# Two transformer blocks on one core: in the second mixer every second weight split, and the row operations after two norms, go from VectorE to GpSimd

## The chip, the cores and the metric

The kernel runs on one core of one Trainium2 chip. The metric is device time in microseconds from start to end of one execution, as the median of several runs; lower is better. The profile's own rows give times from the start of its span.

## The reference

Two blocks work on one sequence of 256 tokens of width 1024, in float32, with batch 1 and one layer each. The first has a mixer of sliding-window attention and a chunked mLSTM, then a gated feed-forward of hidden width 2816. The second, in which the change lies, is cut here to what matters:

```python
x = layer_norm(x, emb_ln_g, emb_ln_b)
sh1, sc1, gt1, sh2, sc2, gt2 = split(silu(c) @ w_ada + b_ada, 6)
h = x * (1 + sc1) + sh1
p = h @ w_in
y_a = gmlp_spatial_gating(p[..., :1024], ...)      # gelu, norm, a 128 x 128 mix over tokens
y_b = rwkv7_time_mix(p[..., 1024:], ...)           # 8 heads, a state update per token
x = layer_norm(ALPHA * x + gt1 * (concat(y_a, y_b) @ w_out), ln1_g, ln1_b)
h = x * (1 + sc2) + sh2
gu = h @ w_ffn_in
x = layer_norm(ALPHA * x + gt2 * ((silu(gu_left) * gu_right) @ w_ffn_out), ln2_g, ln2_b)
```

## The kernel before, in words

**Products in three parts.** Every large product is made exact to nearly float32 by splitting both operands into a high and a low part and adding three matmuls (mm3: high by high, high by low, low by high). The activations are split once; the weights stream in from memory in slots of 128 partitions by 1024 columns (512 KB).

**What happens to a slot (load, lines 787 to 813).** SyncE issues the transfer into one of six buffers named raw. ScalarE casts raw to the high part whi (line 809). VectorE subtracts, wlo = raw - whi (line 810). Then raw is free, and both parts go to TensorE. There are three places for whi and wlo; some phases add places in other tiles (there the high and low parts are named wx, xhi and xlo). stream (line 826) keeps two slots loaded ahead of the job that is emitted. Before the plan starts, the first mixer has its own split (line 422) that the change does not touch.

**The order of work.** From the end of the first mixer on, the order on all engines is written out at build time by a planner (Plan, from line 68). Every instruction is given a cost (cost, line 279), threads have ranks, and each engine is given the instruction of lowest rank among those ready at the simulated time. A planned instruction is never interrupted, and on the chip each engine runs its list strictly in that order, so that one that must wait holds up all behind it on its engine. The splits have level 5 (on engines other than TensorE), the threads of the second mixer 1 to 3, the norms that carry the residual 0 to 0.5, the row operations 5. The planner books an elementwise operation on VectorE at 0.06 us and on GpSimd at 0.44 us, plus one column per 1/960 us on either. Every instruction that is emitted through the planner is shown by the profile at line 376.

**The second mixer (phase "m2").** set_phase gives the phase its name after the last matmul of the first feed-forward has been emitted. From then on the stream splits what is left of four value slots, then three slots of the low-rank gates (one of 256 columns), four of k and r for each of two head groups, four of v, four of the gate branch (gmlp), eight of w_out and the first ones of the next feed-forward's w_ffn_in. Two threads run the recurrence of one head group each: rwkv_pre, rwkv_gram, rwkv_base (a 16 x 16 substitution of 15 steps on VectorE, whose blocks go through memory as "images" on SyncE's queue), rwkv_levels, rwkv_state and rwkv_out. A third, gmlp, may only start at the event m2.x.

**The row operations (row_affine, line 1055).** After a norm, the next product needs only the normalised x, with gain and bias folded into the modulation. The residual needs x times gain plus bias itself; row_affine does that afterwards, two blocks of 128 tokens by two halves of 512 columns by a multiplication and an addition: eight instructions on VectorE. It runs twice: after the embedding norm in the second mixer (it starts when the r of the second head group is there and sets m2.x at its end), and after the norm ln1 at the start of the second feed-forward (it sets f2.x, which the gate's thread and the last norm's rows wait for).

**GpSimd before the change.** It holds the reciprocal square roots of all norms (rsq, a power of -0.5 on a few columns: rms_r, ln_r, hr_r), masks at setup, clears of small tiles and the transfers of rows that are copied to all partitions (brow, sgrow, mix, lora).

Of the kernel before, what the change touches and what calls it, by code (L numbers as in the profile page):

```python
# [8 lines left out]
F32 = mybir.dt.float32  # L9
# [4 lines left out]
ALU = mybir.AluOpType  # L14
# [19 lines left out]
class Pool:  # L34
# [3 lines left out]
    def __init__(self, pool, **bufs):  # L38
        self.pool, self.bufs = pool, bufs
# [349 lines left out]
class Builder:  # L389
    def __init__(self, tc, io, out):  # L390
        self.tc, self.nc, self.io, self.out = tc, tc.nc, io, out
        self.plan = None


    def bg_add(self, job, rate):
# [391 lines left out]
    def load(self, view, kt, cols, place):  # L787

        nc, n = self.nc, kt * cols
        raw = self.wraw.tile([P, n], F32, tag="raw", name="raw")  # L790
        self.plan.level = 5
        nc.sync.dma_start(raw.rearrange("p (k n) -> p k n", k=kt), view)
        cut = [slice(i, min(n, i + 512)) for i in range(0, n, 512)]
        if place in ("x", "t2"):
            pairs = []
            for c in cut:
                hi, lo = (self.ph.tile([P, 512], F32R, tag=place, name="x" + s) for s in ("hi", "lo"))
                nc.scalar.copy(hi, raw[:, c])
                nc.vector.tensor_tensor(lo, raw[:, c], hi.bitcast(F32), op=ALU.subtract)
                pairs.append((hi, lo))  # L800
            self.plan.drop(raw)
            self.plan.level = None
            return pairs, place
        if place == "hT":
            t = self.act.tile([P, 2, 1024], F32R, tag="hT", name="wx")
            hi, lo = t[:, 0, 0:n], t[:, 1, 0:n]
        else:
            hi, lo = (self.wsp.tile([P, n], F32R, tag=s, name=s) for s in ("whi", "wlo"))
        nc.scalar.copy(hi, raw)
        nc.vector.tensor_tensor(lo, raw, hi.bitcast(F32), op=ALU.subtract)  # L810
        self.plan.drop(raw)
        self.plan.level = None
        return [(hi[:, c], lo[:, c]) for c in cut], place
# [241 lines left out]
    def row_affine(self, gb, ev):  # L1055
        for b in range(NB):
            for h in range(2):
                s = slice(h * 512, (h + 1) * 512)
                for i, op in enumerate((ALU.mult, ALU.add)):
                    self.nc.vector.tensor_tensor(self.x[:, b, s], self.x[:, b, s], gb()[i][:, s], op=op)  # L1060
                yield
        self.plan.set(ev)

# [1374 lines left out]
```

## Time and profile before

| | |
|---|---|
| median of 3 runs | 831.02 us (830.13 to 833.05) |
| profiled execution | 836.26 us, its span 834.5 us |
| instructions in the span | 14958 |
| TensorE matmul busy | 784.6 us (94%) |
| TensorE weight load busy | 674.4 us (81%) |
| VectorE (DVE) busy | 581.3 us (70%), 1032 instructions |
| ScalarE (ACT) busy | 379.8 us (46%), 599 instructions |
| GpSimd (POOL) busy | 63.3 us (8%), 143 instructions |
| mean granted TensorE clock | 0.975 of full |
| moved from memory | 175.06 MB, 213 GB/s over the span |

The profile shows one execution; its time is a little above the median of the runs without a profile. An engine's busy time doesn't say whether anything waited for it: that is read from the chain of work that ended last and from the waits. Names in a row stand as out<-in; buffer numbers are left out, and digits in names of inputs too (in_ln_g is ln1_g_2 or ln2_g_2).

### The profile page before, as it was taken

What the parts mean: (1) busy time and instruction counts of PE and PEld (TensorE: products, weight loads), DVE (VectorE), ACT (ScalarE), POOL (GpSimd) and SP (SyncE); (2) the same over time, 40 slices, a digit from 0 to 9 for tenths busy, and PEclk for the clock granted to TensorE, in tenths of its full rate; (3) what the DMA queues carried; (4) which work ended last, traced back from release to release, by engine and by line L of the source; (5) the groups of instructions that cost most, each with busy time, mean ns of one, the idle gap of its engine ahead of it and who ended that gap; (6) DMA issues with size and microseconds to landing.
All of it is one profiled execution on the core that took longest, in us unless ns stands there. A gap on an engine that the chain in (4) does not pass through costs nothing.

```text
span 834.5 us, 14958 instructions
## 1 busy us (share of the span) xinstructions
PE 784.6 (94%) x5912; PEld 674.4 (81%) x5912; DVE 581.3 (70%) x1032; ACT 379.8 (46%) x599; POOL 63.3 (8%) x143
## 2 busy tenths in 40 slices
PE   5999899999979999999998999998897999999995
PEld 4778467899857999998875878876675899999884
DVE  3468866877678977876456467988549778667446
ACT  4346854454554444445425574443235444445330
POOL 3014010100020310000001011000101000000000
PEclk9999999999989999999999999999997999999999
DMA  9996489796759999997659618677434769966711
GB/s 273 318 280 179 159 290 281 208 247 179 245 160 307 272 307 262 305 303 243 186 168 261 165 51 199 155 232 219 153 103 156 219 191 293 251 200 202 254 51 51
DMA packets 205078, 178.94 MB, mean 214 GB/s; under 512 B 24052, under 2 KB 171712, under 8 KB 205008
## 3 DMA queue, kind: packets, MB, share of 16 engines
q1 hardware_dynamic: 201456, 168.37, 69.8%
q0 software_dynamic: 3552, 9.63, 3.5%
q8 instruction: 46, 0.75, 0.4%
q14 instruction: 24, 0.20, 0.1%
HBM read 175.06 MB, written 2.90 MB: 213 GB/s over the span
## 4 chain that ended last, share of the span: by engine, by line
PE 78%; DVE 8%; DMA 5%; ACT 3%; issue 3%; POOL 2%; SPq 1%; DVEq 0%; ACTq 0%; POOLq 0%
PE mm L376 51%; PE sm L376 6%; PE mm L434 4%; PE mm L435 4%; PE mm L436 4%; DMA raw<-in_w_in_dram 2%; PE ad L554 1%; DVE x L376 1%; POOL hr_r L376 1%; DMA base<-image 1%; PE ad L376 1%; DMA ada_raw<-in_w_ada_dram 1%; SPq L376 1%; DMA raw<-in_w_ffn_gate_dram 1%; DVE wlo L376 1%
## 5 line engine op out<-in xcount | busy, mean ns | idle before, releaser
L376 DVE TENSOR_TENSOR wlo<-raw,whi 128x1024 fp32r<-128x1024 f32 (+1 forms) x135 | 164.0, 1218 | 103.2 <-ACT whi L376 102.3
L376 ACT CAST whi<-raw 128x1024 fp32r<-128x1024 f32 (+1 forms) x135 | 140.9, 1045 | 190.3 <-PE mm L376 153.6
L376 PE MATMUL mm<-f_lo,whi 128*128 128x256 f32 x560 | 156.8, 280 | 0.0
L376 PE MATMUL mm<-f_hi,wlo 128*128 128x256 f32 x560 | 156.5, 279 | 0.0
L376 PE MATMUL mm<-f_hi,whi 128*128 128x256 f32 x560 | 156.1, 279 | 0.0
L376 PEld LDWEIGHTS mm<-f_lo,whi 128*128 128x128 f32 x560 | 105.9, 189 | 0.6 <-issue 0.5
L376 PEld LDWEIGHTS mm<-f_hi,whi 128*128 128x128 f32 x560 | 105.5, 188 | 0.3 <-issue 0.2
L376 PEld LDWEIGHTS mm<-f_hi,wlo 128*128 128x128 f32 x560 | 105.2, 188 | 0.7 <-issue 0.7
L427 DVE TENSOR_TENSOR wlo<-raw,whi 128x1024 fp32r<-128x1024 f32 x42 | 51.3, 1220 | 24.2 <-ACT whi L426 24.2
L426 ACT CAST whi<-raw 128x1024 fp32r<-128x1024 f32 x42 | 44.0, 1049 | 45.4 <-DMA raw<-in_w_in_dram 21.1
L434 PE MATMUL mm<-h_hi,whi 128*128 128x256 f32 (+1 forms) x184 | 52.8, 287 | 0.8 <-ACT qkv L1390 0.8
L436 PE MATMUL mm<-h_hi,wlo 128*128 128x256 f32 (+1 forms) x184 | 51.5, 280 | 0.0
L435 PE MATMUL mm<-h_lo,whi 128*128 128x256 f32 (+1 forms) x184 | 51.5, 280 | 0.0
L376 PE MATMUL mm<-m_hi,wlo 128*128 128x256 f32 (+1 forms) x152 | 43.2, 289 | 0.2
L376 PE MATMUL mm<-m_hi,whi 128*128 128x256 f32 (+1 forms) x152 | 42.9, 286 | 0.3 <-DVE kT L376 0.3
L376 PE MATMUL mm<-m_lo,whi 128*128 128x256 f32 (+1 forms) x152 | 42.6, 283 | 0.4 <-DVE vT L376 0.4
L434 PEld LDWEIGHTS mm<-h_hi,whi 128*128 128x128 f32 (+1 forms) x184 | 34.4, 187 | 3.1 <-ACT qkv L1390 1.7
L435 PEld LDWEIGHTS mm<-h_lo,whi 128*128 128x128 f32 (+1 forms) x184 | 34.1, 186 | 0.5 <-issue 0.5
L436 PEld LDWEIGHTS mm<-h_hi,wlo 128*128 128x128 f32 (+1 forms) x184 | 34.2, 186 | 0.0
L376 DVE SCALAR_TENSOR_TENSOR part<-ada_raw,cs,part 128x512 f32<-128x512 f32 x42 | 31.4, 748 | 0.6
L376 PE MATMUL mm<-wlo,hid_hi 128*128 128x512 f32 x80 | 31.3, 391 | 0.0
L376 PE MATMUL mm<-whi,hid_hi 128*128 128x512 f32 x80 | 31.2, 390 | 0.0
(548 smaller groups left out, 1784.0 us busy)
## 6 DMA issues: line engine op xcount, KB each, us to landing
ada_raw<-in_w_ada_dram SPq DMA_DIRECT2D x96, 512.0 KB, 6.0
raw<-in_w_in_dram SPq DMA_DIRECT2D x60, 512.0 KB, 5.4
raw<-in_w_ffn_in_dram SPq DMA_DIRECT2D x44, 512.0 KB, 5.0
raw<-in_w_ffn_gate_dram SPq DMA_DIRECT2D x22, 512.0 KB, 6.0
raw<-in_w_ffn_up_dram SPq DMA_DIRECT2D x22, 512.0 KB, 6.0
raw<-in_w_ffn_down_dram SPq DMA_DIRECT2D x22, 512.0 KB, 5.8
raw<-in_w_ffn_out_dram SPq DMA_DIRECT2D x22, 512.0 KB, 4.1
raw<-in_w_out_dram SPq DMA_DIRECT2D x16, 512.0 KB, 4.3
```

The costliest lines, as they stand in the source:

```text
L376: return lambda *args, **kw: self.plan.issue(self.name, op, args, kw, lambda: f(*args, **kw))
L426: self.nc.scalar.copy(hi, raw)
L427: self.nc.vector.tensor_tensor(lo, raw, hi.bitcast(F32), op=ALU.subtract)
L434: mm(out, lhsT=l[0], rhs=r[0], start=start, stop=False)
L435: mm(out, lhsT=l[0], rhs=r[1], start=False, stop=False)
L436: mm(out, lhsT=l[1], rhs=r[0], start=False, stop=stop)
L554: nc.tensor.matmul(ps[32 * g:32 * g + 32, :], lhsT=cv["rep"][:, 2 * (s - 1) + g, :], rhs=raws[s - 1 + g // 2][:, g % 2, :], start=s == 1, ...
```

## The change

Two lines change their engine. In load, a flag self.odd turns over at every slot of the ordinary kind that is split while the phase is "m2", beginning with true; where it is true, GpSimd does the subtraction, elsewhere VectorE as before. Outside that phase the flag is false. In row_affine all eight operations of both norms go to GpSimd. The planner sees the new engine and books it by its own cost, so the written order of all engines may differ from the one before.

```diff
     def __init__(self, tc, io, out):
         self.tc, self.nc, self.io, self.out = tc, tc.nc, io, out
-        self.plan = None
+        self.plan, self.odd = None, False
...
         nc.scalar.copy(hi, raw)
-        nc.vector.tensor_tensor(lo, raw, hi.bitcast(F32), op=ALU.subtract)
+
+        self.odd = self.phase == "m2" and not self.odd
+        (nc.gpsimd if self.odd else nc.vector).tensor_tensor(lo, raw, hi.bitcast(F32), op=ALU.subtract)
         self.plan.drop(raw)
...
                 for i, op in enumerate((ALU.mult, ALU.add)):
-                    self.nc.vector.tensor_tensor(self.x[:, b, s], self.x[:, b, s], gb()[i][:, s], op=op)
+                    self.nc.gpsimd.tensor_tensor(self.x[:, b, s], self.x[:, b, s], gb()[i][:, s], op=op)
                 yield
```

## Rows read from the trace of the kernel before

**Rows 1.** Busy by stretch: stretch, length, each engine's us (instructions), clock, DMA share, GB/s.
```profile
439.00:640.00 201.00, 182.21 (x1751) 147.11 (x1744) 139.78 (x309) 89.92 (x162) 18.62 (x21) 0.96 0.60 166
640.00:835.00 195.00, 185.47 (x1239) 168.71 (x1237) 131.07 (x162) 77.37 (x95) 3.86 (x6) 0.98 0.65 193
```

**Rows 2.** The page: chain that ended last, share of the span by engine.
```profile
PE 78%; DVE 8%; DMA 5%; ACT 3%; issue 3%; POOL 2%; SPq 1%; DVEq 0%; ACTq 0%; POOLq 0%
```

**Rows 3.** The chain's pieces in the mixer (start, us, what), and its line for 540:580.
```profile
by line: SPq L376 14.2%; DMA raw<-in_w_out_dram 12.8%; PE sm L376 11.9%; DVE vv L376 8.2%; PE mm L376 7.8%; DVE gl_t L376 6.7%; issue 6.3%; DVE wlo L376 6.1%; PE ad L376 5.4%; ACT whi L376 5.3%; DVE base L376 4.4%; DVE W L376 3.5%; ACT gl_t
...
489.73 2.61 POOL hr_r L376
...
560.04 1.05 ACT whi L376
561.12 1.23 DVE wlo L376
```

**Rows 4.** Waits in 439 to 640: who waited for whom, us, times, longest.
```profile
DVE wlo L376 <- ACT whi L376: 19.9, 13, 4.2
...
PE sm L376 <- DVE x L376: 4.8, 2, 2.8
PE sm L376 <- ACT rx L376: 4.1, 4, 1.6
```

**Rows 5.** Groups on VectorE in 439 to 640; last, the row operations of both norms.
```profile
L376 DVE TENSOR_TENSOR wlo<-raw,whi 128x1024 fp32r<-128x1024 f32 (+1 forms) x31 | 37.0, 1196 | 19.9 <-ACT whi L376 19.9
...
L376 DVE TENSOR_TENSOR x<-x,brow 128x512 f32<-128x512 f32 x8 | 5.4, 692 | 0.0
...
L376 DVE TENSOR_TENSOR x<-x,brow x16: 674/689/704, 529.6 to 659.0; 128x512 f32<-128x512 f32 x16
```

**Rows 6.** GpSimd in order of time: start, us, instruction, in brackets the idle before.
```profile
285.93 0.67 POOL L376 TENSOR_SCALAR_AFFINE_SELECT w_s<-w_s 128x512 f32<-128x512 f32 x1
...
445.94 1.48 POOL L376 TENSOR_TENSOR ln_r<-ln_ve,mhalf 128x1 f32<-128x1 f32 x1 [3.83 <-DVE ln_ve L376]
...
631.27 0.56 POOL L376 TENSOR_TENSOR ln_r<-ln_ve,mhalf 128x1 f32<-128x1 f32 x1 [18.51 <-DVE ln_ve L376]
638.85 1.40 POOL L376 TENSOR_TENSOR ln_r<-ln_ve,mhalf 128x1 f32<-128x1 f32 x1 [7.02 <-DVE ln_ve L376]
```

**Rows 7.** VectorE in order of time.
```profile
285.66 1.49 DVE L376 SCALAR_TENSOR_TENSOR hid_lo<-th,hid_hi 128x512 fp32r<-128x512 f32 x1
...
506.00 2.36 DVE L376 TENSOR_TENSOR wlo<-raw,whi 128x1024 fp32r<-128x1024 f32 x2
...
547.28 0.68 DVE L376 TENSOR_TENSOR x<-x,brow 128x512 f32<-128x512 f32 x1
...
549.33 0.43 DVE L376 TENSOR_SCALAR gl_t<-gl_t 128x512 f32<-128x512 f32 x1 [0.38 <-ACT gl_t L376]
...
638.62 1.21 DVE L376 TENSOR_TENSOR wlo<-raw,whi 128x1024 fp32r<-128x1024 f32 x1
...
677.12 0.68 DVE L376 SCALAR_TENSOR_TENSOR hid_lo<-th,hid_hi 128x512 fp32r<-128x512 f32 x1
```

**Rows 8.** ScalarE in order of time.
```profile
496.30 1.04 ACT L376 CAST whi<-raw 128x1024 fp32r<-128x1024 f32 x1
...
628.82 2.94 ACT L376 CAST whi<-raw 128x1024 fp32r<-128x1024 f32 x3 [5.78 <-PE mm L376]
```

**Rows 9.** Busy by stretch, start of the second feed-forward.
```profile
635.00:645.00 10.00, 8.03 (x26) 5.98 (x27) 9.53 (x21) 7.51 (x17) 2.63 (x3) 0.61 0.73 212
645.00:655.00 10.00, 10.00 (x45) 8.15 (x45) 9.41 (x12) 5.07 (x6) 0.00 (x0) 1.00 0.89 270
```

**Rows 10.** Busy by stretch, two stretches of the mixer.
```profile
545.00:595.00 50.00, 43.62 (x672) 32.78 (x671) 38.52 (x93) 18.10 (x33) 4.54 (x6) 0.97 0.79 242
515.00:545.00 30.00, 29.53 (x297) 25.93 (x296) 28.17 (x78) 13.03 (x28) 0.00 (x0) 1.00 0.75 174
```

## The prediction

> **What bounds the kernel now.** I read the stretches first [rows 1]. The second mixer runs from about 439 to 640 us. TensorE is busy there for 182.2 of 201.0 us, VectorE for 139.8, ScalarE for 89.9 and GpSimd for 18.6. So TensorE sets the pace, with 18.8 us of holes; the last stretch, the second feed-forward, has 9.5 us of them. Whatever the change does, it can give back at most the holes of the mixer and those at the start of the feed-forward.
>
> Then the chain of work that ended last [rows 2]: 78% of the span is TensorE, 8% VectorE, 2% GpSimd. Its pieces inside the mixer [rows 3] show a reciprocal root on GpSimd (hr_r, 2.61 us) and a weight slot's cast on ScalarE with the subtract on VectorE behind it. Between 540 and 580 us the VectorE entries that its line names (vv, gl_t, wlo, base, W) add up to 28.9%: there VectorE has what TensorE waits for.
>
> Third, the waits [rows 4]. VectorE stood idle 19.9 us in the mixer because its next instruction was a slot's subtract and ScalarE's cast had not come: 13 times, the longest 4.2 us. Everything behind it in VectorE's order waited too. TensorE itself hardly waits for a low part: its longest entries are the norm's x (4.8 us) and rx (4.1 us), the copy of what hr_r gives.
>
> Fourth, the groups on VectorE [rows 5]: 31 subtracts cost 37.0 us and are its largest group by far (one of 256 columns, the rest of 1024 at 1.22 us); the eight row operations on x cost 5.4 us. Over both norms these are 16, the first at 529.6, the last at 659.0, of 0.69 us each.
>
> **What is moved.** The slots split while the phase is "m2" are, in job order: the fourth value slot, three low-rank slots, eight of k and r, four of v, four of the gate branch, eight of w_out, and three of the next feed-forward: 31 by the kernel's lists. The flag turns true at the first of them, so 16 go to GpSimd, all 1024 wide, and 15 stay. The earlier value slots are loaded before the phase is set and stay too. row_affine serves two norms: eight operations in the mixer and eight at the start of the feed-forward. So VectorE loses 16 x 1.22 + 8 x 0.69 = 25.0 us in the mixer, and 8 x 0.69 = 5.5 us after it.
>
> **What it costs on GpSimd.** The trace has no wide operation with two inputs there. The nearest rows are VectorE's own 1.22 us (lower end) and GpSimd's affine_select on w_s with 0.67 us for 512 columns and one input [rows 6]: twice the columns make 1.34 us, and twice the inputs on top 2.7 us (upper end). I take 2.0, the middle of the two that the row on the same engine gives, for a slot, and half, 1.0, for a row operation: 16 x 2.0 + 8 x 1.0 = 40 us in the mixer, 8 us after it. With 18.6 us busy now, GpSimd has the room. The planner, which fixes the order of every engine, books 0.44 + 1024/960 = 1.51 us, so it is half a microsecond too hopeful. The Trainium skill, GPSIMD Engine Reference, section "Performance versus the Vector engine", measures a two-input operation at 1.96 times VectorE's; that would make 2.4 us a slot and 48 us in all, and no run here shows it yet.
>
> **The two engines exclude each other.** This decides the sign. A small root (ln_r) takes 0.56 us at 631.27 [rows 6], but 1.40 us at 638.85, when it starts inside the subtract of 638.62 [rows 7]: it ends some 0.4 us after the subtract does. The 1.48 us at 445.94 looks like the same. The other way round there is one row: hid_lo, two inputs in SBUF, 512 columns, takes 0.68 us at 677.12 and 1.49 us at 285.66, when the affine_select of 285.93 runs through it. So a GpSimd operation that reads SBUF holds up a VectorE one with two inputs there, and for its whole length as far as this row shows. VectorE is busy 70% of the mixer [rows 1]; roughly half of that time is such work (my reading of the operand names: raw, whi, x, brow, vv, base against sm and mm, which are PSUM). So of GpSimd's 40 us I charge a share of 0.35, which is 14 us, to VectorE; the bounds are 0 and 40. Net relief: 25.0 - 14 = 11 us.
>
> What of it lies on the path? VectorE holds 8% of the whole chain and 29% of it between 540 and 580. I take 0.15 over the mixer, nearer the first because most of the mixer looks like the whole: 11 x 0.15 = **-1.7 us**. The idle time in front of subtracts goes by half with the 16 slots, 10 us, at the same 0.15: **-1.5 us**. A GpSimd that has nothing else to do also takes a slot earlier: the cast of 496.30 [rows 8] ended at 497.3, its subtract on VectorE began only in the row of 506.00 [rows 7]. The raw buffer then comes free earlier and SP issues the next transfer earlier; TensorE did not wait for either, so I count nothing. If that lead went, a slot would come 0.8 us later than now.
>
> **GpSimd's own queue.** It has 24 long entries more in the mixer, and the roots of the norms stand behind them in order. The first slot of the feed-forward is cast by about 629.8, a third into the row of 628.82 [rows 8]; its 2.0 us on GpSimd reach past 631.27, where ln_r of the last norm's first half starts, and the whole way to the next matmul stands behind that root: **+1.0 us** (bounds 0 and 2.7). The root at 638.85 loses the subtract beside it, 1.40 to 0.56: **-0.8 us**. The one at 445.94 gains 0.9 if it comes before its neighbour slot and waits 1.1 if after: nothing. The DMAs issued from that queue (sgrow, mix, brow) are fetched microseconds before their use.
>
> **The feed-forward's start.** From 635 to 655 VectorE is busy 9.5 and 9.4 of 10 us [rows 9], almost only with two-input subtracts whose slots TensorE takes as they come. The eight row operations ran until 659, between and behind the subtracts. On GpSimd they start right after the second root and run from about 640 to 648, across them. Blocking 8 x 1.0 x 0.95 = 7.6 us against 5.5 us of relief leaves VectorE 2 us later; half of it reaches TensorE: **+1.0 us** (bounds -1 and +5).
>
> Sum: -1.7 - 1.5 + 1.0 - 0.8 + 1.0 = **-2.0 us**. The profiled execution took 836.26 us (span 834.5), 5.2 above the median of 831.02; it would come to 834.3, and the median to **829.0 us**. A difference under 0.3% (2.5 us) can hardly be told from none here, so my point lies just inside "no change".
>
> **Rivals.**
> 1. *VectorE gets free where it is full, and the gate branch moves forward.* gmlp may not start before the row operations are done; its first operation on VectorE (gl_t, 549.33) follows the last row operation (547.28) [rows 7]. On GpSimd they would be done near 528. Then gmlp's work leaves 549 to 576, where it is interleaved with base, X, W and G of the second head group. For it: TensorE has 6.4 us of its holes between 545 and 595 [rows 10]. Against it: from 515 to 545, where that work would go, VectorE is busy 28.2 of 30 us. Price: 6.4 us at most in place of the 3.2 above, the +1.2 of the queue and the feed-forward as before: -5.2, **826 us**. Chance 0.28.
> 2. *The port is the new wait.* Every GpSimd operation stops VectorE in full, because its next two-input operation is always close: 40 us of blocking against 25 of relief in the mixer, 15 us of VectorE more, first in front of base (515 to 530), whose image transfers stand in SP's queue ahead of the second head group's. At the 0.29 of the chain 4.4 us, and 2.6 us, half the bound, at the feed-forward's start: +7, **838 us**. It decides from the point where more than 25 of the 40 us are charged to VectorE (a share of 0.62 against my 0.35). For it: the hid_lo row. Against it: PSUM-fed work fills half of VectorE. The Trainium skill, SBUF — State Buffer, section "Who interferes with whom", states just this: a VectorE instruction with two SBUF inputs contends with a GpSimd one that reads SBUF, and the second to issue blocks fully. The hid_lo row agrees with 1.49 against 0.68 us; how often it strikes is open. Chance 0.30.
> 3. *Only the order changes.* The planner re-sorts all engines, and relief and delay both fall into TensorE's cover: **831 us**. Chance 0.07.
>
> My forecast has the remaining 0.35.
>
> **How the numbers follow.** The forecast's own width is about 3 us to each side: of its 0.35, 0.14 falls beyond -0.3%, 0.17 within, 0.04 above. Rival 1 gives 0.27 faster and 0.01 same; rival 2 0.28 slower and 0.02 same; rival 3 0.01, 0.05 and 0.01. Together faster 0.42, same 0.25, slower 0.33. The range goes from 6 us under rival 1 (all bounds at their best: no queueing, no blocking) to 2 us over rival 2: 820 to 840, which leaves out the ends where GpSimd takes 2.7 us a slot and blocks in full. The likeliest case alone would be 826 to 832.
>
> **What would show it.** The groups: 16 subtracts of 1024 columns on GpSimd at 1.3 to 2.7 us, 16 row operations at 0.7 to 1.4. VectorE's busy time in the mixer down from 139.8 by 25 us; if blocking counts as busy, by 11, with two-input rows of 1.22 and 0.69 us stretched to 2 and 1.5. The idle time behind whi on VectorE halves from 19.9. ln_r near 631 starts late. The first gl_t comes before 545. I am wrong if TensorE's holes in the mixer move by more than 5 us, or if GpSimd takes over 2.7 us a slot.

## The result, and the profile after

The changed kernel takes **856.03 us** (median of four runs, 854.83 to 858.84), the kernel before beside it 831.62 us: a ratio of 1.0299, 95% interval 1.0267 to 1.033. It is 24 us slower; 829.0 had been forecast and 840 was the end of the range.

Busy time by stretch, after (columns as in [rows 1]; the first of the four residual additions (res) that close the second mixer came at 625.38 us before and comes at 635.96 now):

```profile
439.00:640.00 201.00, 180.10 (x1710) 145.05 (x1707) 128.42 (x263) 82.01 (x147) 60.39 (x41) 0.94 0.58 162
515.00:535.00 20.00, 14.48 (x110) 12.78 (x109) 19.09 (x35) 5.92 (x9) 15.96 (x10) 0.91 0.46 118
635.00:655.00 20.00, 10.88 (x41) 7.97 (x40) 18.14 (x27) 8.54 (x14) 10.17 (x7) 0.75 0.49 161
```

and the two short stretches of the kernel before:

```profile
515.00:535.00 20.00, 19.62 (x194) 17.18 (x193) 18.20 (x58) 7.26 (x15) 0.00 (x0) 1.00 0.80 201
635.00:655.00 20.00, 18.03 (x70) 14.14 (x71) 18.94 (x32) 12.58 (x22) 2.63 (x3) 0.81 0.81 241
```

TensorE has two new holes. In each of these stretches it was busy over 18 of 20 us, and is now busy 14.5 and 10.9. VectorE is as full as ever there (18 to 19 of 20 us), but gets 35 and 27 instructions done instead of 58 and 32 (the same stretch of time does not hold quite the same work: the moved instructions are gone from it, and the rest has shifted). With the holes TensorE's granted clock is lower (0.91 for 1.00, 0.75 for 0.81), a mean between its two levels of 1.2 and 2.4 GHz.

Busy time on the page, first the kernel before, then the changed one:

```profile
PE 784.6 (94%) x5912; PEld 674.4 (81%) x5912; DVE 581.3 (70%) x1032; ACT 379.8 (46%) x599; POOL 63.3 (8%) x143
```
```profile
PE 788.8 (92%) x5912; PEld 675.5 (79%) x5912; DVE 584.6 (68%) x1000; ACT 381.1 (45%) x599; POOL 123.7 (14%) x175
```

VectorE lost 32 instructions and gained 3.3 us. The 32 are worth 16 x 1.22 + 16 x 0.69 = 30.5 us [rows 5], so what stayed has been stretched by 584.6 - (581.3 - 30.5) = **33.8 us**. TensorE is busy 4.2 us longer for the same 5912 matmuls, at a mean granted clock of 0.965 in place of 0.975; the rest of the 19.9 us by which the span grew is idle time. (The profiled execution of the kernel before was some 5 us above its median, so the two spans lie less far apart than the medians.)

GpSimd's new groups:

```profile
L376 POOL TENSOR_TENSOR wlo<-raw,whi 128x1024 fp32r<-128x1024 f32 x15 | 37.5, 2499 | 93.1 <-ACT whi L376 93.1
```
```profile
445.01 2.41 POOL L376 TENSOR_TENSOR wx<-raw,wx 128x1024 fp32r<-128x1024 f32 x1
...
518.91 7.11 POOL L376 TENSOR_TENSOR x<-x,brow 128x512 f32<-128x512 f32 x5
528.25 3.72 POOL L376 TENSOR_TENSOR wlo<-raw,whi 128x1024 fp32r<-128x1024 f32 x1 [2.22 <-ACT whi L376]
...
651.10 12.88 POOL L376 TENSOR_TENSOR x<-x,brow 128x512 f32<-128x512 f32 x8
```

A slot takes 2.4 us (2.50 in the mean, one of them 3.72), a row operation 1.3 to 1.7 (16 in 23.3 us): 63.2 us in all. The Trainium skill (GPSIMD Engine Reference, "Performance versus the Vector engine") gives 1.96 as the ratio of GpSimd's time to VectorE's for a two-input addition of 2048 columns. Here the slot of 445.01 took 2.41 us against VectorE's 1.22, a ratio of 1.98; for a row operation of 512 columns it is 1.46 (23.3 / 16) against 0.69, or 2.1.

Now VectorE's groups from 439 to 660 us that the change did not touch, before:

```profile
L376 DVE TENSOR_TENSOR base<-base 64x1 f32<-64x1 f32 (+14 forms) x30 | 8.7, 291 | 0.9 <-DMA base<-image 0.8
L376 DVE TENSOR_REDUCE base<-base 64x1 f32<-64x1 f32 (+14 forms) x30 | 6.8, 227 | 0.2
...
L376 DVE TENSOR_SCALAR x<-x,ln_mv,ln_r 128x512 f32<-128x512 f32 x6 | 3.0, 543 | 0.9 <-POOL ln_r L376 0.9
...
L376 DVE SCALAR_TENSOR_TENSOR ss<-rT,cols,kf 128x256 f32<-128x256 f32 x4 | 1.8, 476 | 0.0
...
L376 DVE SCALAR_TENSOR_TENSOR ar<-PP,kk 128x256 f32<-128x256 f32 x4 | 1.7, 413 | 0.0
...
L376 DVE TENSOR_SCALAR vv<-vv,ln_mv,ln_r 128x512 f32<-128x512 f32 x2 | 1.1, 536 | 0.0
```

and after:

```profile
L376 DVE TENSOR_TENSOR base<-base 64x1 f32<-64x1 f32 (+14 forms) x30 | 13.5, 451 | 0.4
L376 DVE TENSOR_SCALAR x<-x,ln_mv,ln_r 128x512 f32<-128x512 f32 x6 | 9.0, 1540 | 1.1 <-POOL ln_r L376 1.1
L376 DVE TENSOR_REDUCE base<-base 64x1 f32<-64x1 f32 (+14 forms) x30 | 6.7, 225 | 0.4
L376 DVE SCALAR_TENSOR_TENSOR ss<-rT,cols,kf 128x256 f32<-128x256 f32 x4 | 5.8, 1477 | 0.0
...
L376 DVE SCALAR_TENSOR_TENSOR ar<-PP,kk 128x256 f32<-128x256 f32 x4 | 3.8, 946 | 0.0
...
L376 DVE TENSOR_SCALAR vv<-vv,ln_mv,ln_r 128x512 f32<-128x512 f32 x2 | 3.2, 1587 | 0.0
```

The same instructions take one and a half times (base) to three times as long. They are not any instructions: ss and ar lead to base, which leads to everything of a head group; the normalisation of x leads to the next product. The normalisation of x and that of vv have one tensor as input, and are held up like those with two. The reductions of base in between, with one input as well, keep their time (227 and 225 ns). How one hold-up comes about is seen in order of time, VectorE first, then GpSimd:

```profile
444.26 0.15 DVE L376 TENSOR_SCALAR ln_ve<-ln_mv 128x1 f32<-128x1 f32 x1
445.08 3.08 DVE L376 TENSOR_SCALAR x<-x,ln_mv,ln_r 128x512 f32<-128x512 f32 x2 [0.66 <-POOL ln_r L376]
```
```profile
444.50 0.55 POOL L376 TENSOR_TENSOR ln_r<-ln_ve,mhalf 128x1 f32<-128x1 f32 x1 [3.83 <-DVE ln_ve L376]
445.01 2.41 POOL L376 TENSOR_TENSOR wx<-raw,wx 128x1024 fp32r<-128x1024 f32 x1
```

The root on GpSimd lets VectorE's normalisation go, and GpSimd's next instruction, the slot, starts 0.07 us sooner than that normalisation and holds it up by 2.08 us: 3.08 us for the pair of halves, which took 1.00 before. The same meets the norm at the feed-forward's start (3.01 us at 644.18, beside the slot of 644.11). TensorE's waits in 438 to 670 us, after:

```profile
PE sm L376 <- DVE x L376: 11.1, 4, 6.1
PE mm L376 <- ACT f_hi L376: 4.8, 2, 2.7
PE sm L376 <- DVE base L376: 4.0, 2, 2.9
...
PE mm L376 <- POOL wlo L376: 1.4, 3, 0.6
```

It waits for x (11.1 us against 4.8 in [rows 4]) and for base (not among the longest before), and hardly for what GpSimd makes. The idle time of VectorE in front of the subtracts fell to 14.9 us from 22.5 in the same window: that relief came, and the kernel is slower all the same.

### The profile page after: what moved, and what is told of

Read it like the earlier page. It is cut to its first block, busy times and chain, and to the rows that moved or that the text cites. A ratio compares the mean times of both kernels' runs of the same rounds, so it can differ in the third digit from the quotient of the medians.

```text
span 854.4 us, 14961 instructions
## 1 busy us (share of the span) xinstructions
PE 788.8 (92%) x5912; PEld 675.5 (79%) x5912; DVE 584.6 (68%) x1000; ACT 381.1 (45%) x599; POOL 123.7 (14%) x175
## 5 line engine op out<-in xcount | busy, mean ns | idle before, releaser
L376 DVE TENSOR_TENSOR wlo<-raw,whi 128x1024 fp32r<-128x1024 f32 x120 | 147.7, 1233 | 103.3 <-ACT whi L376 102.0
L427 DVE TENSOR_TENSOR wlo<-raw,whi 128x1024 fp32r<-128x1024 f32 x42 | 51.3, 1220 | 31.8 <-ACT whi L426 31.7
L376 POOL TENSOR_TENSOR wlo<-raw,whi 128x1024 fp32r<-128x1024 f32 x15 | 37.5, 2499 | 93.1 <-ACT whi L376 93.1
L376 POOL TENSOR_TENSOR rms_r<-rms_m,mhalf 128x1 f32<-128x1 f32 x6 | 4.2, 693 | 218.1 <-DVE rms_m L376 218.1
L376 POOL TENSOR_TENSOR ln_r<-ln_ve,mhalf 128x1 f32<-128x1 f32 x8 | 5.9, 738 | 201.9 <-DVE ln_ve L376 198.4
```

Source lines behind the costliest of these rows:

```text
L376: return lambda *args, **kw: self.plan.issue(self.name, op, args, kw, lambda: f(*args, **kw))
L427: self.nc.vector.tensor_tensor(lo, raw, hi.bitcast(F32), op=ALU.subtract)
```

## The experiments

Four explanations stand against each other: the two engines exclude each other (port theory), GpSimd's latency and queue, the planner's new order of all engines, and a mixture. Each run stood beside runs of the kernel before on the same chip (medians 831.25 to 832.94). In the table, VectorE's busy time is that of the profiled execution.

| run | order of | moved operations done by | us | ratio, 95% interval | VectorE busy |
|---|---|---|---|---|---|
| before | before | VectorE | 831.6 | 1 | 581.3 |
| changed | after | GpSimd | 856.0 | 1.0299, 1.0267 to 1.033 | 584.6 |
| e1 | its own | GpSimd, rows only | 837.4 | 1.0051, 1.002 to 1.0082 | 579.9 |
| e2 | its own | GpSimd, slots only | 849.3 | 1.0178, 1.0122 to 1.0235 | 581.5 |
| e3 | after | VectorE | 849.2 | 1.0191, 1.0153 to 1.0229 | 582.2 |
| e4 | before | GpSimd | 849.1 | 1.0186, 1.0136 to 1.0236 | 582.7 |
| e5 | after | GpSimd fills | 833.9 | 1.0018, 0.9996 to 1.004 | 559.0 |
| e6 | before | GpSimd fills | 835.4 | 1.0037, 0.9999 to 1.0075 | 559.5 |
| e7 | before | VectorE; GpSimd reads on top | 846.5 | 1.0172, 1.0138 to 1.0207 | 603.1 |
| e8 | its own | GpSimd | 867.5 | 1.0412, 1.0366 to 1.0457 | 580.3 |
| e9 | after | GpSimd, real in the mixer | 849.1 | 1.0226, 1.0165 to 1.0287 | 576.7 |
| e10 | after | GpSimd, real at the feed-forward | 841.0 | 1.013, 1.0071 to 1.0189 | 567.1 |
| e11 | of e8 | GpSimd fills | 846.1 | 1.0175, 1.0114 to 1.0235 | 557.8 |
| e12 | after | GpSimd, real slots, filled rows | 843.9 | 1.0145, 1.0099 to 1.019 | 571.7 |

### e1 and e2: one line of the change each

e1 keeps the row operations on GpSimd, e2 the slots; the other line goes back to VectorE.

```diff
-        (nc.gpsimd if self.odd else nc.vector).tensor_tensor(lo, raw, hi.bitcast(F32), op=ALU.subtract)
+        nc.vector.tensor_tensor(lo, raw, hi.bitcast(F32), op=ALU.subtract)
```

> Only the 16 row operations on GpSimd, all subtracts on VectorE. Port theory (a GpSimd operation that reads SBUF stops VectorE's two-input and its SBUF-to-SBUF copy-like instructions): the row operations stand before base and at the feed-forward's start, where VectorE is full; 843 to 850, more than half of the loss. Order theory (the planner's new order is the loss, the engine is not): near 831, because nothing is said of this order; any value. Queue theory (work waits in GpSimd's own list): 832 to 836, only the roots and the row transfers behind the row operations are late.

> Only the 16 subtracts on GpSimd, the row operations on VectorE. Port theory: 836 to 843, the smaller part, since the subtracts come singly and often beside work fed from PSUM. Queue theory: 840 to 848, the larger part, because slots at 2.5 us and the norms' roots stand in one list. If both parts only add, the two excesses make 24 us together.

Measured 837.43 and 849.32: the first between the two theories, the second above both. Each of the two has an order of its own, so 4 and 15 us are not yet the shares that the two lines have in the changed kernel (e12 gives those). e2 also shows the exclusion the other way round, GpSimd first, then what VectorE did meanwhile:

```profile
538.15 7.50 POOL L376 TENSOR_TENSOR wlo<-raw,whi 128x1024 fp32r<-128x1024 f32 x1 [10.43 <-ACT whi L376]
```
```profile
538.08 0.69 DVE L376 TENSOR_TENSOR x<-x,brow 128x512 f32<-128x512 f32 x1
538.67 0.46 DVE L376 TENSOR_TENSOR base<-base 64x169 f32<-64x169 f32 x1
...
540.89 1.23 DVE L376 TENSOR_TENSOR wlo<-raw,whi 128x1024 fp32r<-128x1024 f32 x1
...
543.48 0.38 DVE L376 TENSOR_REDUCE base<-base 64x15 f32<-64x225 f32 x1
```

VectorE was first and went on with one SBUF operation right behind the other, 11 of them until 543.86; GpSimd's subtract, 2.4 us long elsewhere, ended 1.8 us after the last. None of VectorE's eleven is stretched. TensorE waited 5.7 us for this low part, the longest of three such waits:

```profile
PE mm L376 <- POOL wlo L376: 6.5, 3, 5.7
```

### e3 and e4: the order and the engine taken apart

The planner books one engine and the other executes. e3 has the changed kernel's order with VectorE doing all the work, e4 the old order with GpSimd doing the 32 operations.

```diff
+    def on(self, booked, real, *args, **kw):
+        f = getattr(self.nc.nc, real).tensor_tensor
+        return self.plan.issue(booked, "tensor_tensor", args, kw, lambda: f(*args, **kw))
...
+            self.on("vector", "gpsimd", lo, raw, hi.bitcast(F32), op=ALU.subtract)
```

> The order of the changed kernel (the planner books the 32 instructions on GpSimd), but VectorE executes them. Port or queue theory: the loss goes, 826 to 836. Order theory: the loss stays, 846 to 858.

> The order of the kernel before (the planner books VectorE), but GpSimd executes the 32 instructions. Port or queue theory: slow although the order is the old one, 845 to 860. Order theory: 828 to 836.

Measured 849.24 and 849.08. The old order on GpSimd loses 17 us, as the port theory and the queue theory have it; but the new order on VectorE loses 17 us as well, which both exclude. Together they don't add up (24, not 34). e3 is an ambiguous run: in it VectorE does 30 us of work that its order was laid out without, so it tests an order together with a load that it was not made for. These two alone settle nothing; the next pair settles more.

### e5 and e6: the same waits and the same time on GpSimd, without reading

In place of each moved operation GpSimd does one column of it, so that every wait stays, and then fills the rest twice with a constant. Left out are the low parts of 16 slots and x after the two norms.

```diff
+    def quiet(self, booked, out, a, b, op):
+        g, n = self.nc.nc.gpsimd, out.shape[-1]
+
+        def call():
+            g.tensor_tensor(out[:, 0:1], a[:, 0:1], b[:, 0:1], op=op)
+            for _ in range(2):
+                g.memset(out.bitcast(F32)[:, 1:n], 0.5)
+        return self.plan.issue(booked, "tensor_tensor", (out, a, b), {"op": op}, call)
```

> The changed kernel's order on every engine. In place of each of the 32 moved operations GpSimd does one column of it (so that all waits stay) and then fills the rest twice with a constant, which takes time on its queue but reads nothing; the low parts of 16 slots and x after the two norms are left out. If two thirds or more of the loss is GpSimd's reading of SBUF holding up VectorE, this comes to 831 to 845 us: the order's share alone, less VectorE's 30 us of relief. If the order and GpSimd's latency and queue make the loss, it stays at 848 to 858. VectorE's normalise beside the slot near 644 falls from 3.0 back to about 1.0 us under the first theory.

> The kernel before's order on every engine, GpSimd filling in place of each moved operation as in the run before this one. Port theory: the 17 us of the run with the old order on GpSimd are nearly all the two engines' exclusion, so this comes to 828 to 836. Queue and latency theory: 842 to 852, since GpSimd takes as long and the roots stand behind it as they did there.

GpSimd is as full as in the changed kernel (117.4 us on the page against 123.7), a filled slot takes 2.1 us and a filled row operation 1.6:

```profile
L401 POOL MEMSET wlo<- 128x1023 f32 x30 | 28.7, 958 | 0.9
L401 POOL MEMSET x<- 128x511 f32 x32 | 16.9, 528 | 0.9
L399 POOL TENSOR_TENSOR x<-x,brow 128x1 f32<-128x1 f32 x16 | 8.9, 557 | 0.0
...
L399 POOL TENSOR_TENSOR wlo<-raw,whi 128x1 fp32r<-128x1 f32 x15 | 3.2, 212 | 85.9 <-ACT whi L376 85.9
```

**The loss is gone: 833.9 us in the new order, 835.4 in the old one.** With the same order, the same waits and nearly the same time on GpSimd, what the reading costs is 856.0 - 833.9 = 22.1 of the 24 us; in the old order 849.1 - 835.4 = 13.7 of 17. (These are differences of medians, here and below; by the ratios they come out up to 2 us different, 23.4 and 12.4 here.) What is left is 1.5 us in the one and 3 in the other, at the edge of what can be told from zero. It is a net: the order, GpSimd's latency and its queue on one side, the 30.5 us lifted off VectorE on the other. e5's profiled execution took 825.92 us, the shortest of its eleven; I read from it how long instructions take, and no more than roughly the waits. VectorE's groups in e5, same stretch:

```profile
L376 DVE TENSOR_TENSOR base<-base 64x1 f32<-64x1 f32 (+14 forms) x30 | 8.7, 291 | 1.9 <-DMA base<-image 1.5
...
L376 DVE TENSOR_SCALAR x<-x,ln_mv,ln_r 128x512 f32<-128x512 f32 x6 | 6.5, 1127 | 1.2 <-POOL ln_r L376 1.2
...
L376 DVE SCALAR_TENSOR_TENSOR ss<-rT,cols,kf 128x256 f32<-128x256 f32 x4 | 1.7, 480 | 0.0
L376 DVE SCALAR_TENSOR_TENSOR ar<-PP,kk 128x256 f32<-128x256 f32 x4 | 1.7, 419 | 0.0
```

base, ss and ar are back at 291, 480 and 419 ns, the values of before. One part of my expectation failed: the normalisation of x is not back (1127 ns in the mean; the pair at 622.68 takes 2.45 us beside a filled slot). A fill, which only writes, holds up this one-input operation and not those with two inputs. The Trainium skill, SBUF — State Buffer, section "Who interferes with whom", has both halves of this: a VectorE instruction with two SBUF inputs contends with a GpSimd one that reads SBUF and not with one that only writes, while tensor_scalar and copies can enter a mode that takes the shared pair of ports as a whole. These rows agree with it: ss takes 1477 ns beside reads and 480 beside fills; one normalisation takes 0.50 us alone, 1.2 beside a filled slot and 1.5 beside a real one (half of 1.00, 2.45 and 3.08). So e5 still holds a little exclusion: VectorE is busy for 559.0 us, and without any it would be 581.3 - 30.5 = 550.8. TensorE's waits, same window as above, have come about two thirds of the way back, for x (from 11.1 us, 4.8 before) and for base (from 4.0):

```profile
PE sm L376 <- DVE x L376: 7.0, 3, 4.0
...
PE sm L376 <- DVE base L376: 1.4, 2, 1.2
```

e3 fits in with this, though no run tests my reading of it. VectorE's busy time is 582.2 us in e3 and 559.0 in e5 in one and the same order, and the times are 15.3 us apart: in the new order VectorE seems to have no room for that much more, whether it is work (e3) or blocking (the changed kernel, 584.6).

### e7: exclusion with nothing moved

The kernel before, with reading operations of 512 columns on GpSimd on top, whose results nobody takes.

```diff
+            r = v.tensor_tensor(out, a, b, op=op)
+            for s in dup:
+                n = s.shape[-1]
+                g.tensor_tensor(self.spare[:, 0:n], s, s, op=ALU.subtract)
```

> The kernel before, nothing moved: VectorE does all its work in the old order. GpSimd does 64 reading operations of 512 columns on top, two for each of the 16 slots and 32 on x at the norms, into a scratch tile that nobody reads. Nothing waits for their results, but the roots and DMA issues of GpSimd's queue stand behind them, and buffers come free later. Port theory: VectorE loses their length where it is busy, with nothing given back: 840 to 858. Latency theory (the loss is TensorE waiting for low parts that GpSimd makes slower): 831 to 836.

There are 48 such operations in the run, 74.7 us on GpSimd, and not the 64 that the expectation says: 32 on slots and 16 on x. Measured 846.53, +14.3 us by the ratio. Nobody waits for their results, VectorE's work and order are the old ones, and VectorE is busy 603.1 - 581.3 = 21.8 us longer. (The roots behind these operations in GpSimd's queue and the buffers that they read can come later too, so the 14.3 us need not all be VectorE's.) The pieces also show the length of one block: the normalisation beside two back-to-back pieces of 512 columns takes 2.44 us in place of 1.00,

```profile
448.20 2.44 DVE L376 TENSOR_SCALAR x<-x,ln_mv,ln_r 128x512 f32<-128x512 f32 x2 [0.44 <-POOL ln_r L376]
```
```profile
448.14 2.21 POOL L402 TENSOR_TENSOR spare<-wx 128x512 f32<-128x512 f32 x2
```

against 3.08 beside one piece of 1024.

### e8 and e11: the true cost told to the planner

GpSimd's two-input operations are booked at 2.40 and 1.45 us in place of 1.51 and 0.97 (the edit also books the roots, two-input operations on a few columns, at 0.50 in place of 0.44); e11 has the same order with fills.

```diff
         elif engine == "gpsimd":
             cost = 0.44
+            if op == "tensor_tensor":
+                return 0.5, 1.9 * n / 1024
```

> The changed kernel, with GpSimd's two-input operations booked in the planner at what they take (2.40 us for 1024 columns, 1.45 for 512) in place of 1.51 and 0.97. If the new order is bad because it counts on results too early, this takes back a part of the order's 17 us: 838 to 850. If the order is bad for another reason, or the exclusion is what counts, it stays at 850 to 860.

> The order of the run that booked GpSimd's true times (867 us), with fillings in place of all 32 operations. If that order only meets more exclusion, this comes to 830 to 840. If that order is itself a bad one, it stays above 850.

Both missed. The truer booking is worse, 867.5 us, and e11 says why in two parts: 846.1 with fills, 14 to 15 us over the kernel before and 12 over the same fills in the changed kernel's order (833.9), and the reading adds 21.4, as much as in the changed kernel's order (22.1). So one order can cost 12 us more than another here; the changed kernel's is not a costly one. What makes e8's order bad was not followed up.

### e9, e10 and e12: where, and which

A count decides which operations are real and which are fills: e9 the mixer's 14 slots and 8 row operations, e10 the last 2 slots and the second norm's 8 row operations, e12 all slots and no row operation.

```diff
+        self.count[n] = self.count.get(n, 0) + 1
+        late = self.count[n] > (14 if n == 1024 else 8)
+        if not late:
+            return self.nc.gpsimd.tensor_tensor(out, a, b, op=op)
```

> The changed kernel's order. GpSimd does the first 14 subtracts and the first 8 row operations for real (the mixer), and the last 2 subtracts and the second norm's 8 row operations by filling (the low parts of two slots of the feed-forward and x after its norm are left out). The changed kernel was 10.6 us behind the kernel before at the mixer's last residual (res) and 20 us at the feed-forward's f_lo, so if each stall stays with its own place this comes to 841 to 847. If the mixer's stalls are absorbed later, 833 to 839; if the whole loss is the mixer's, 850 to 858.

> The same order, the other way round: the mixer's 14 subtracts and 8 row operations are fillings, the last 2 subtracts and the second norm's 8 row operations real. With each stall in its place: 9 to 11 us over the run with nothing but fillings, 841 to 846. If the feed-forward's start loses only because it comes late and its buffers are late, 832 to 837.

> The changed kernel's order. GpSimd does all 16 subtracts for real, and the 16 row operations by filling (x after the two norms is left out). With the exclusion summed by its length, the subtracts read for 39.9 us of GpSimd's 63.2 us of moved work, 63% of the 22 us between the changed kernel and its order with fillings alone: 845 to 850. If only the norm's normalise beside a slot and the row operations' run of 8 at the feed-forward matter, 838 to 843.

Over e5's 833.9 the mixer's reading costs 15.2 us and the feed-forward's 7.1: 22.3 together, and 22.1 was to be explained (by the ratios 17.3 and 9.3 for 23.4). The mixer's part is more and the feed-forward's less than I had read from the two traces, but the two add up within what is measured, so neither seems to be absorbed by the other. By kind, the slots cost 10.0 us (843.9, between the two expectations) and the row operations are left with the other 12.1, though those are only 23.3 of the 63.2 us. That is a difference: real row operations with filled slots were not run, and in an order of its own (e1) the kernel with real row operations lost only 4 us. They come as runs of five, three and eight across the recurrence's start and the feed-forward's start. In e10 the eight last:

```profile
640.11 12.87 POOL L376 TENSOR_TENSOR x<-x,brow 128x512 f32<-128x512 f32 x8
```
```profile
642.19 2.90 DVE L376 TENSOR_SCALAR x<-x,ln_mv,ln_r 128x512 f32<-128x512 f32 x2
...
645.02 5.14 DVE L376 TENSOR_TENSOR xlo<-raw,xhi 128x512 fp32r<-128x512 f32 x3
```

Three subtracts of 512 columns, some 0.68 us each elsewhere, take 5.14 us, and every one is a weight part that TensorE takes as it comes.

## Why the prediction was wrong

**GpSimd's duration.** Forecast 2.0 and 1.0 us, measured 2.50 and 1.46 in the mean: inside the bound of 2.7 for a slot (one, of 3.72, was not), above the 1.4 at which I had set the top for a row operation. 63.2 us in place of 48. The factor of 1.96 in the Trainium skill (GPSIMD Engine Reference, "Performance versus the Vector engine"), which the prediction gives, would have had the slots right (the 48 us worked out from it there are those of the mixer; with the eight row operations after it they are 57.6).

**The blocking share.** I had charged 14 us in the mixer and 7.6 at the feed-forward's start, 21.6 in all; measured 33.8, a share of 0.54 of the 63.2. A little over half of the miss is the duration (at the old share of 21.6/48 = 0.45 the 63.2 us alone make 28.4); the rest is the share, in which I had counted only two-input operations. The normalisations, with one input (543 to 1540 and 536 to 1587 ns), make 6.0 + 2.1 = 8.1 of the 33.8 us. The Trainium skill, SBUF — State Buffer, section "Who interferes with whom", which I named for rival 2, says that tensor_scalar can contend too; I had left that out.

**The step that failed** is none of these sizes but "11 x 0.15": one weight for what is lifted off VectorE and for what is put on it, laid on their difference (and in the same way the half at the feed-forward's start). With the measured blocking the net would have been 33.8 - 30.5, three us more on VectorE, and by 0.15 or 0.29 at most 1 us more. What is put on weighs far more: 25.6 us more VectorE from e5 to the changed kernel cost 22.1, 0.86 us each; in e7 21.8 cost 14.3, 0.66 each. What is lifted has shown no gain: in e6 VectorE is 21.8 us less busy in the old order and the time does not fall (1.0037). But that is a net as well, 30.5 us lifted and 8.7 put on by the fills, with GpSimd's latency on top. At 0.66 to 0.86 the 8.7 alone would cost 5.7 to 7.5 us, and the time is 3.1 up, so that the lifting may have been worth some 3 to 4 us, about 0.1 for each us lifted (an estimate from e6 and e7; no run lifts without putting on). That is near my 0.15: the weight was wrong for what is put on. The waits say why the two differ. TensorE hardly waits for a low part, in the kernel before as in the changed one (1.4 us); what the exclusion strikes is whatever VectorE happens to do at that moment, and x and base, for which TensorE waits 11.1 and 4.0 us in the changed kernel, are among it. The 8% and 29% of the chain measure VectorE as a whole and can't tell the one from the other.

**The idle time in front of subtracts**, -1.5 us: it fell by 7.6 us (22.5 to 14.9 in 438 to 670) where 10 had been forecast. In e6 it fell to 16.6, and the time did not fall with it, so that no gain of its own can be seen.

**GpSimd's queue.** Place and sign right: the first slot of the feed-forward (640.62, 2.55 us) ends as the root starts (643.14), and the other root has lost its neighbour (0.56 us at 650.58 in place of 1.40). At 445 I had set "nothing": the root gains (0.55), and the slot that moved behind it stands on the normalisation, 2.08 us lost; the same at 644.18. In both cases I had looked at the order of slot and root, and not at who runs beside the slot once the root lets VectorE go.

**The feed-forward's start**, +1.0 us with bounds of -1 and +5: the place was right, the eight row operations do run across VectorE's subtracts; they and two slots cost 7.1 us (e10), beyond the bound. With 12.88 us for the eight in place of 8 the forecast's own formula, half of 12.88 x 0.95 - 5.5, would give 3.4, so the length explains a part; the weight of a half and the slot on the normalisation are left for the rest, and no run tells them apart. One reading there was off as well: in [rows 9] VectorE's time is not almost only subtracts; in order of time these are some 13 of its 18.9 us.

**The rivals.** Rival 2 had the mechanism and, at 0.30, a little less of a chance than my forecast; its price, 15 us more of VectorE at 0.29, had more VectorE time than was measured (3 us net) at a weight far too low; it fell short by the same mistake, and with it the range's upper end. Rival 1's early gate branch came (the first gl_t at 539.50 us after 549.33 [rows 7], in e5 even at 525.42) and bought nothing that can be seen: e5, where little is in its way, is at 833.9 and not at 826. Rival 3 fits the changed kernel's order (e5), though e11 shows that an order can cost.

## What to carry to other kernels

Before work goes from VectorE to GpSimd, list what VectorE does while GpSimd would read SBUF: if dependent chains of SBUF operations run there (a recurrence, a norm), each GpSimd instruction of 2.4 us can land on them. Here each us by which VectorE was stretched cost 0.66 to 0.86 us, while 30 us taken off it showed no gain. Weigh the two sides separately, by what TensorE waits for in the trace, and not by VectorE's share of the chain. Where the suspicion is exclusion, replace the suspect's body by fills of the same length and keep its waits: order and queue stay, and the difference is what the reading costs.

## What the runs showed that I had not expected

- GpSimd can be starved, too: a 2.4 us subtract took 7.50 us (e2) while VectorE ran eleven SBUF instructions back to back, none of them stretched. The Trainium skill, SBUF — State Buffer, "Who interferes with whom", says that who issues first holds the ports for its instruction; here the loser did not get them when the first one ended: by its usual 2.4 us it ran only near the end of VectorE's run.
- A fill on GpSimd, which reads nothing, holds up VectorE's one-input normalisation (1.00 to 2.45 us for a pair) and leaves its two-input operations alone (ss 480 ns).
- VectorE 22 us less busy showed no gain in the old order (e6), although TensorE's longest wait in the kernel before is for VectorE [rows 4].
- A planner told the true cost of an engine wrote an order that is 12 us worse with the same work (e11 against e5: 846.1 and 833.9 us); why stays open.
